# Attention in four-head units on a TensorE-bound decoder trunk: scores of even and odd heads in turn, and first loads in finer steps

## The chip, the cores and the metric

The kernel runs on one core of a Trainium2 chip. The metric is the device time of one execution in microseconds; the profile's span, from the first to the last instruction of the program, is a little shorter. TensorE does matmuls and transposes, VectorE (DVE) and ScalarE (ACT) do elementwise work, GpSimd (POOL) does a few powers and issues some DMAs, and SyncE (SP) issues nearly all loads.

## The reference

Two layers of a decoder trunk on 256 tokens of width 2048. Each layer normalises its input, projects it once, feeds the columns to a gated spatial unit (A) and to windowed attention (B), projects both back, and then runs a SwiGLU block:

```python
def swa_sink_attention(q, k, v, q_norm_g, k_norm_g, sinks, rel_bias):
    ...
    scores = jnp.einsum('bnqkgd,bnskd->bnkgqs', q, kb).astype(jnp.float32) * scale
    ...
    scores = jnp.where(valid[None, :, None, None], scores + bias, NEG_INF)
    sink = ...
    probs = jax.nn.softmax(jnp.concatenate([scores, sink], axis=-1), axis=-1)[..., :-1]
    out = jnp.einsum('bnkgqs,bnskd->bnqkgd', probs.astype(vb.dtype), vb)
...
for l in range(DEPTH):
    h = rms_norm(x, norm1_g[l])
    z = h @ w_in[l]
    z_sgu = jax.nn.gelu(z[..., :2 * SGU_WIDTH], approximate=False)
    out_a = chunked_sgu(z_sgu, sgu_norm_g[l], sgu_w[l], sgu_b[l])
    out_b = swa_sink_attention(...)
    mixed = jnp.concatenate([rms_norm(out_a, out_norm_a[l]),
                             rms_norm(out_b, out_norm_b[l])], axis=-1)
    x = x + mixed @ w_out[l]
    h2 = rms_norm(x, norm2_g[l])
    x = x + (jax.nn.silu(h2 @ w_gate[l]) * (h2 @ w_up[l])) @ w_down[l]
```

Attention has 16 query heads of width 64 in 4 key groups of 4 heads, and two query blocks of 128 tokens. The first block sees 128 keys, the second 256. Everything is float32.

## The kernel before

**The weight stream.** Every product takes its weights in tiles of 256 x 512 floats. SP loads a tile into `raw` (line 90), ScalarE casts it to a rounded high part `wh` (line 99), VectorE computes the rest `wl` (line 100), and TensorE makes three matmuls of 512 columns per part (`mm3`, lines 138 to 140). One such tile with its 12 matmuls is a *unit*, and a counter `clock[0]` advances by one tick per unit. All other work is put into the stream with `later(delay, fn)`, which runs `fn` once the counter has advanced far enough. So the order of the Python calls, refined by the scheduler that builds the program, sets the order on each engine.

**PSUM.** There are eight banks. `pa` has five, for the accumulators `acc` (each product uses two, one per token block). `pd` has two and `pm` one; small results (transposes, scores, probabilities) take a bank through `small_ps`, which goes round over `pm`, `pd`, `pd`.

**Attention.** In each layer the projection is done in blocks of 512 columns: keys and values first, then the first eight query heads (`in_block(4)`), then the others (`in_block(5)`), then the gate columns (`v_gate`, `u_gated`). From `in_block(5)` on, the stream carries attention between its units. There are 12 attention units per layer: for each key group one with the first query block and all four heads, one with the second block and the even heads (`par` = (0,)), and one with the second block and the odd heads. `attend` makes the scores (line 361), adds the bias into `s` (line 368), takes the maximum (373), the exponentials with their sums on ScalarE (381) and the reciprocal of the sum. Three ticks later `turn` transposes the probabilities into `pt` (lines 395 and 396), five ticks later `weigh` multiplies them with the values (line 402) into `ob` (line 412). `attend_end` transposes `ob` for the output projection. Even heads lie in partitions 0 to 63 and odd heads in partitions 64 to 127 of `qT` and `kT`, so a score matmul has 64 rows:

```python
nc.tensor.matmul(
    ps[:, i, :],
    qT[h // 8][HD * r : HD * r + HD, (h % 8) // 2, t * P : (t + 1) * P],
    kT[HD * r : HD * r + HD, g, :nk],
    start=True, stop=True,
)
```

**The spatial gate.** `v_gate` normalises v per head: squares and sums on VectorE, the power on POOL (`inv_rms`, line 186), and the products on VectorE again (lines 456 and 457), which wait for POOL.

**The start.** TensorE runs 12 matmuls on a constant tile (`heat`, line 169). SP first issues the constants `cst` (line 164), then two tiles of the transposed input (`first_pair`, line 241), then the first weights in halves.

Of the kernel before, what the change touches and what calls it, by code (L numbers as in the profile page):

```python
# [12 lines left out]
F32 = mybir.dt.float32  # L13
# [3 lines left out]
ALU = mybir.AluOpType  # L17
# [4 lines left out]
P = 128  # L22
# [4 lines left out]
HD = 64  # L27
NH = 16
NKV = 4
GRP = NH // NKV  # L30
# [6 lines left out]
KT = D // P  # L37
# [30 lines left out]
def trunk(ctx, tc, x, xt, w_in, w_out, w_gate, w_up, w_down, sgu_w, sgu_g, consts,  # L68
          rel_bias, onehot, radd, out):
    nc = tc.nc  # L70
# [4 lines left out]
    zp = ctx.enter_context(tc.tile_pool(name="zp", bufs=8))  # L75
    ap = ctx.enter_context(tc.tile_pool(name="ap", bufs=2))
    sp = ctx.enter_context(tc.tile_pool(name="sp", bufs=4))
    dp = ctx.enter_context(tc.tile_pool(name="dp", bufs=1, space=DRAM))
    pa = ctx.enter_context(tc.tile_pool(name="pa", bufs=5, space=PSUM))
    pd = ctx.enter_context(tc.tile_pool(name="pd", bufs=2, space=PSUM))  # L80
    pm = ctx.enter_context(tc.tile_pool(name="pm", bufs=1, space=PSUM))
# [36 lines left out]
    def later(delay, fn):  # L118
        pending.append((clock[0] + delay, next(serial), fn))
# [11 lines left out]
    turns = itertools.count()  # L131

    def small_ps(shape, name):
        pool, tag = ((pm, "sm"), (pd, "dacc"), (pd, "dacc"))[next(turns) % 3]
        return pool.tile(shape, F32, tag=tag, name=name)

    def mm3(acc, ah, al, wh, wl, first, last):
# [23 lines left out]
        return acc  # L161

    cst = cp.tile([P, L, C_L], F32, tag="cst", name="cst")
    nc.sync.dma_start(cst, consts)
    junk = zp.tile([P, NB], BF16, tag="z", name="junk")
    nc.vector.memset(junk, 1.0)
    heat = small_ps([P, NB], "heat")
# [6 lines left out]
    ident = cp.tile([P, P], F32, tag="ident", name="ident")  # L174
    make_identity(nc, ident)

    def small(shape, name):
        return sp.tile(shape, F32, tag=name, name=name)
# [15 lines left out]
    def split_gain(ps, lay, col, tag, spare=False):  # L194
        pair = pair_tile(tag, spare)
        for j in range(2):
            g = cst[:, lay, col + j : col + j + 1]
            nc.scalar.activation(pair[:, 0, j, :], ps[:, j, :], AF.Copy, scale=g)
            nc.vector.scalar_tensor_tensor(
                pair[:, 1, j, :], ps[:, j, :], g, f(pair[:, 0, j, :]), ALU.mult, ALU.subtract  # L200
            )
        return pair

    def transpose_pair(blocks, ps=None):
        ps = small_ps([P, 2, SEQ], "ps_t") if ps is None else ps
        for j in range(2):
            for t in range(NTOK):
                nc.tensor.transpose(
                    ps[:, j, t * P : (t + 1) * P], blocks[t][:, j * P : (j + 1) * P], ident
                )  # L210
        return ps

    def sum_sq(dst, src):
        void = zp.tile([P, NB], BF16, tag="z", name="void")
        nc.scalar.activation(void[:, : src.free_size()], src, AF.Square, accum_out=dst)
# [15 lines left out]
    def bc(a, n):  # L231
        return a.unsqueeze(2).to_broadcast([P, a.shape[1], n])
# [6 lines left out]
    def first_pair(p, pairs=pairs1):  # L239
        xr = zp.tile([P, 2, SEQ], F32, tag="z", name="xr")  # L240
        nc.sync.dma_start(xr, xt[:, 2 * p : 2 * p + 2, :])
        pairs.append(split_gain(xr, 0, C_G1 + 2 * p, "hT"))
# [22 lines left out]
        )  # L265
        nc.sync.dma_start(rdram, skew)

    for p in range(2):
        first_pair(p)
    for p in range(2, KT // 2):  # L270
        later(p - 1, lambda p=p: first_pair(p))
    for i in range(2 * NTOK):
        later(5 + 2 * i, lambda i=i: load_x(i // 2, i % 2))
    later(11, rel_table)
# [1 line left out]
    for lay in range(L):  # L276
        layer = {}

        def in_block(nb, lay=lay, pairs=pairs1):
            return product([w_in[lay, nb, c] for c in range(KT // 2)], pairs)  # L280
# [7 lines left out]
        zkv = []  # L288
        kT = ap.tile([P, NKV, SEQ], F32, tag="big", name="kT", bufs=8)

        def kv_norm(acc, lay=lay, layer=layer, zkv=zkv, kT=kT):
# [22 lines left out]
        qT = [  # L314
            ap.tile([P, 4, SEQ], F32, tag="big", name=f"qT{b}", bufs=8) for b in range(2)
        ]
# [22 lines left out]
        ob = {}  # L339
        bias = {}  # L340
        pairs_b = [None] * NKV

        def load_bias(g, bias=bias):
            bt = ap.tile([P, GRP, SEQ], F32, tag="big", name="bias", bufs=8)
            nc.gpsimd.dma_start(bt, rdram[g * GRP : (g + 1) * GRP].rearrange("h q k -> q h k"))
            bias[g] = bt

        def attend(g, t, par, zkv=zkv, kT=kT, qT=qT, ob=ob, bias=bias, layer=layer):
            nk = (t + 1) * P
            k0 = SEQ - nk  # L350
            nh = 2 * len(par)
            heads = [h for h in range(GRP) if h % 2 in par]
            step = heads[1] - heads[0]
            nkb = nk // P
            nsink = layer["nsink"]
            s = ap.tile([P, nh, nk], F32, tag="spt", name="s", bufs=4)
            for r in par:
                ps = small_ps([P, 2, nk], "ps_s")
                for i in range(2):
                    h = g * GRP + 2 * i + r  # L360
                    nc.tensor.matmul(  # L361
                        ps[:, i, :],
                        qT[h // 8][HD * r : HD * r + HD, (h % 8) // 2, t * P : (t + 1) * P],
                        kT[HD * r : HD * r + HD, g, :nk],
                        start=True,
                        stop=True,
                    )
                nc.vector.scalar_tensor_tensor(
                    s[:, par.index(r) :: len(par), :], ps, 1.0 / math.sqrt(HD),
                    bias[g][:, r::2, k0:], ALU.mult, ALU.add,  # L370
                )
            m = small([P, GRP], "m")[:, :nh]
            nc.vector.tensor_reduce(m, s, AX.X, ALU.max)
            hs = slice(g * GRP + heads[0], (g + 1) * GRP, step)
            nm = small([P, GRP], "nm")[:, :nh]
            nc.vector.scalar_tensor_tensor(nm, m, -1.0, nsink[:, hs], ALU.mult, ALU.min)
            es = small([P, GRP], "es")[:, :nh]
            nc.vector.tensor_tensor(es, nm, nsink[:, hs], ALU.subtract)
            den = small([P, GRP], "den")[:, :nh]
            for i in range(nh):  # L380
                nc.scalar.activation(
                    s[:, i, :], s[:, i, :], AF.Exp, bias=nm[:, i : i + 1],
                    accum_out=den[:, i : i + 1],
                )
            nc.scalar.activation(es, es, AF.Exp)
            rden = small([P, GRP], "rden")[:, :nh]
            nc.vector.tensor_tensor(rden, den, es, ALU.add)
            nc.vector.reciprocal(rden, rden)
            pt = ap.tile([P, nh * nkb, P], F32, tag="spt", name="pt", bufs=4)

            def turn():
                pst = small_ps([P, nh * nkb, P], "ps_p")
                s4 = s.rearrange("p h (b k) -> p (h b) k", k=P)
                for i in range(nh * nkb):
                    nc.tensor.transpose(pst[:, i, :], s4[:, i, :], ident)
                nc.vector.tensor_copy(pt, pst)

            def weigh():
                pv = small_ps([P, nh, HD], "ps_v")
                for i in range(nh):  # L400
                    for b in range(nkb):
                        nc.tensor.matmul(
                            pv[:, i, :],
                            pt[:, i * nkb + b, :],
                            zkv[b][:, (NKV + g) * HD : (NKV + g + 1) * HD],
                            start=b == 0,
                            stop=b == nkb - 1,
                        )
                if (g, t) not in ob:
                    ob[g, t] = zp.tile([P, GRP * HD], F32, tag="z", name="ob")  # L410
                o3 = ob[g, t].rearrange("p (h d) -> p h d", d=HD)
                nc.vector.tensor_tensor(o3[:, heads[0] :: step, :], pv, bc(rden, HD), ALU.mult)

            later(3, turn)
            later(5, weigh)

        def attend_end(g, lay=lay, ob=ob, ssb=ssb, pairs_b=pairs_b):
            for t in range(NTOK):
                sum_sq(ssb[t][:, g : g + 1], ob[g, t])
            ps = transpose_pair([ob[g, t] for t in range(NTOK)])  # L420
            pairs_b[g] = split_gain(ps, lay, C_GB + 2 * g, "aT", g >= 2)
# [106 lines left out]
        acc = in_block(4)  # L528
        load_bias(0)
        q_norm(0, acc)  # L530
        units = [(g, t, par) for g in range(NKV) for t, par in ((0, (0, 1)), (1, (0,)), (1, (1,)))]
        for i, (g, t, par) in enumerate(units):
            at = 6 + (9 * i) // 4
            later(at, lambda g=g, t=t, par=par: attend(g, t, par))
            if i % 3 == 2:
                if g + 1 < NKV:
                    later(at, lambda g=g: load_bias(g + 1))
                later(at + 7, lambda g=g: attend_end(g))
        layer["anchor"] = anchor[0]
        q_norm(1, in_block(5))  # L540
        for b in range(2):
# [276 lines left out]
```

## Time and profile before

| | |
|---|---|
| median of 3 runs | 1976.16 us (1975.98 to 1976.36) |
| the profiled execution | 1975.9 us |
| its span | 1974.1 us |
| TensorE busy | 1958.7 us |
| VectorE busy | 1664.9 us |
| ScalarE busy | 1137.7 us |
| GpSimd busy | 119.2 us |
| moved by DMA | 420.22 MB |

"Busy" is the union of the instructions of an engine; a matmul's end is modelled, and matmuls overlap in the pipeline, so the distance from one start to the next says what one costs, not the duration. A float32 matmul (scores, weighted sums) leaves two records.

### The profile page before, as it was taken

How to read it: one execution, taken by the hardware profiler on the slowest of the kernel's cores; microseconds unless marked ns; L12 is line 12 of the kernel's file. 1: busy time of each engine (PE TensorE's matmuls, PEld its weight loads, DVE VectorE, ACT ScalarE, POOL GpSimd, SP SyncE). 2: the span in 40 equal slices, each digit the busy share in tenths (PEclk: the TensorE clock that was granted, in tenths of full speed). 3: DMA queues.
4: the chain of work that ended last, by engine and by line, in shares of the span. 5: the costliest groups of instructions: out<-in, count | busy, mean ns of one | idle time of the engine just before them, and what ended most of it. 6: DMA issues, size and time to landing. Idle time of an engine off the chain costs nothing.

```text
span 1974.1 us, 24670 instructions
## 1 busy us (share of the span) xinstructions
PE 1958.7 (99%) x8942; PEld 1602.0 (81%) x8942; DVE 1664.9 (84%) x1931; ACT 1137.7 (58%) x1441; POOL 119.2 (6%) x129
## 2 busy tenths in 40 slices
PE   9999999999999999999999999999999999999999
PEld 6788888878878888888888788888888888888887
DVE  6777689989999898999667776899899898999984
ACT  6465566556656556656455655666556565565562
POOL 1211001000000000000002100000000000000000
PEclk9999999999999999999999999999999999999999
DMA  8753557776686776867655445586776867768773
GB/s 315 262 173 129 191 162 229 225 226 212 215 267 197 238 226 206 254 221 244 201 185 194 147 150 187 167 244 202 235 224 223 255 204 234 230 217 255 216 241 110
DMA packets 118554, 420.22 MB, mean 213 GB/s; under 512 B 13040, under 2 KB 15216, under 8 KB 118432
## 3 DMA queue, kind: packets, MB, share of 16 engines
q1 hardware_dynamic: 107072, 377.65, 55.4%
q0 software_dynamic: 11360, 41.00, 11.6%
q8 instruction: 70, 1.15, 0.2%
q14 instruction: 52, 0.43, 0.1%
HBM read 416.47 MB, written 4.23 MB: 213 GB/s over the span
## 4 chain that ended last, share of the span: by engine, by line
PE 87%; DVE 7%; DMA 3%; issue 2%; ACT 1%; POOL 0%; SPq 0%; ACTq 0%; POOLq 0%
PE dacc L138 10%; PE dacc L139 9%; PE dacc L140 9%; PE acc L138 9%; PE acc L140 9%; PE acc L139 9%; PE m L140 6%; PE m L139 6%; PE m L138 6%; DVE wl L100 3%; PE n L138 3%; PE n L140 3%; PE n L139 3%; DMA raw<-in_w_down_dram 1%; PE ps_s L361 1%
## 5 line engine op out<-in xcount | busy, mean ns | idle before, releaser
L99 ACT CAST wh<-raw 128x1024 fp32r<-128x1024 f32 (+1 forms) x770 | 793.8, 1049 | 652.6 <-PE acc L140 156.4
L100 DVE TENSOR_TENSOR wl<-raw,wh 128x1024 fp32r<-128x1024 f32 (+1 forms) x770 | 920.3, 1217 | 190.5 <-ACT wh L99 180.9
L138 PE MATMUL dacc<-wh,aT 128*128 128x512 f32 x576 | 225.1, 393 | 2.8 <-DVE xres L707 2.8
L139 PE MATMUL dacc<-wl,aT 128*128 128x512 f32 x576 | 225.0, 391 | 0.0
L140 PE MATMUL dacc<-wh,aT 128*128 128x512 f32 x576 | 224.8, 390 | 0.0
L139 PE MATMUL m<-wl,ext 128*128 128x512 f32 x512 | 200.6, 392 | 1.0 <-DVE wl L100 1.0
L138 PE MATMUL m<-wh,ext 128*128 128x512 f32 x512 | 200.1, 391 | 0.4 <-ACT wh L99 0.4
L140 PE MATMUL m<-wh,ext 128*128 128x512 f32 x512 | 199.4, 389 | 0.0
L138 PE MATMUL acc<-wh,hT 128*128 128x512 f32 x448 | 180.0, 404 | 1.0 <-ACT wh L99 1.0
L139 PE MATMUL acc<-wl,hT 128*128 128x512 f32 x448 | 175.4, 392 | 0.3 <-DVE wl L100 0.2
L140 PE MATMUL acc<-wh,hT 128*128 128x512 f32 x448 | 175.6, 392 | 0.0
L99 ACT CAST wh<-t 128x1024 fp32r<-128x1024 f32 x128 | 134.8, 1053 | 49.3 <-PE dacc L140 26.3
L100 DVE TENSOR_TENSOR wl<-t,wh 128x1024 fp32r<-128x1024 f32 x128 | 155.9, 1218 | 8.2 <-ACT wh L99 5.3
L138 PE MATMUL dacc<-wh,hT 128*128 128x512 f32 x384 | 151.2, 394 | 0.7 <-ACT sg L682 0.4
L138 PE MATMUL acc<-wh,aT 128*128 128x512 f32 x384 | 151.3, 394 | 0.0
L140 PE MATMUL acc<-wh,aT 128*128 128x512 f32 x384 | 149.9, 390 | 0.0
L140 PE MATMUL dacc<-wh,hT 128*128 128x512 f32 x384 | 149.7, 390 | 0.0
L139 PE MATMUL dacc<-wl,hT 128*128 128x512 f32 x384 | 149.7, 390 | 0.0
L139 PE MATMUL acc<-wl,aT 128*128 128x512 f32 x384 | 149.6, 390 | 0.0
L624 POOL DMA_DIRECT2D t<-in_w_gate_dram x64 | 54.6, 853 | 1335.7 <-DVE wl L100 767.3
L138 PEld LDWEIGHTS dacc<-wh,aT 128*128 128x128 f32 x576 | 107.7, 188 | 27.8 <-DVE xres L707 5.6
L139 PEld LDWEIGHTS dacc<-wl,aT 128*128 128x128 f32 x576 | 108.2, 188 | 22.9 <-DVE wl L100 0.8
(151 smaller groups left out, 3007.5 us busy)
## 6 DMA issues: line engine op xcount, KB each, us to landing
raw<-in_w_gate_dram SPq DMA_DIRECT2D x176, 512.0 KB, 5.5
raw<-in_w_up_dram SPq DMA_DIRECT2D x176, 512.0 KB, 4.5
raw<-in_w_down_dram SPq DMA_DIRECT2D x176, 512.0 KB, 4.6
raw<-in_w_in_dram SPq DMA_DIRECT2D x108, 512.0 KB, 4.5
raw<-in_w_out_dram SPq DMA_DIRECT2D x64, 512.0 KB, 3.3
t<-in_w_gate_dram POOLq DMA_DIRECT2D x64, 512.0 KB, 7.1
bias<-rdram POOLq DMA_DIRECT2D x8, 512.0 KB, 5.8
xr<-in_xt_dram SPq DMA_DIRECT2D x8, 256.0 KB, 5.6
```

The lines of the kernel that those rows point to most:

```text
L99: nc.scalar.copy(wh[:, j : j + step, :], src)
L100: nc.vector.tensor_tensor(wl[:, j : j + step, :], src, f(wh[:, j : j + step, :]), ALU.subtract)
L138: nc.tensor.matmul(acc, ah, wh, start=first, stop=False)
L139: nc.tensor.matmul(acc, ah, wl, start=False, stop=False)
L140: nc.tensor.matmul(acc, al, wh, start=False, stop=last)
L361: nc.tensor.matmul(ps[:, i, :], qT[h // 8][HD * r : HD * r + HD, (h % 8) // 2, t * P : (t + 1) * P], kT[HD * r : HD * r + HD, g, :nk], sta ...
L624: nc.gpsimd.dma_start(t2, w_gate[lay, b, i, 1], accum_op=ALU.add)
```

## The change

Four things change. `small_ps` goes round over four turns, the third of which takes one of the five accumulator banks. The constants are loaded from ScalarE's queue, and only the first input tile is issued ahead of the first weights; the others follow one per tick. Attention has 8 units per layer: a key group and a query block, always with all four heads; the score matmuls go through the heads in the order even, odd, even, odd, into a bank for each parity, and the bias is added after all four. The transposes of the second block are split into two steps one tick apart, and its weighted sum comes at 6 ticks. Times within the stream are set anew, and the bias of the next group is loaded two to three ticks sooner.

```diff
     def small_ps(shape, name):
-        pool, tag = ((pm, "sm"), (pd, "dacc"), (pd, "dacc"))[next(turns) % 3]
+        pool, tag = ((pm, "sm"), (pd, "dacc"), (pa, "acc"), (pd, "dacc"))[next(turns) % 4]
...
-    nc.sync.dma_start(cst, consts)
+    nc.scalar.dma_start(cst, consts)
...
-    for p in range(2):
-        first_pair(p)
-    for p in range(2, KT // 2):
-        later(p - 1, lambda p=p: first_pair(p))
+    first_pair(0)
+    for p in range(1, KT // 2):
+        later(p, lambda p=p: first_pair(p))
...
-        def attend(g, t, par, ...):
+        def attend(g, t, ...):
-            s = ap.tile([P, nh, nk], F32, tag="spt", name="s", bufs=4)
-            for r in par:
-                ps = small_ps([P, 2, nk], "ps_s")
-                for i in range(2):
+            s = ap.tile([P, GRP, nk], F32, tag="spt", name="s", bufs=4)
+            halves = [small_ps([P, 2, nk], "ps_s") for r in range(2)]
+            for i in range(2):
+                for r in range(2):
                     h = g * GRP + 2 * i + r
                     nc.tensor.matmul(
-                        ps[:, i, :],
+                        halves[r][:, i, :],
...
+            for r in range(2):
                 nc.vector.scalar_tensor_tensor(
-                    s[:, par.index(r) :: len(par), :], ps, 1.0 / math.sqrt(HD),
-                    bias[g][:, r::2, k0:], ALU.mult, ALU.add,
+                    s[:, r::2, :], halves[r], 1.0 / math.sqrt(HD), bias[g][:, r::2, k0:],
+                    ALU.mult, ALU.add,
                 )
...
-            def turn():
-                pst = small_ps([P, nh * nkb, P], "ps_p")
+            def turn(c):
+                pst = small_ps([P, GRP, P], "ps_p")
                 s4 = s.rearrange("p h (b k) -> p (h b) k", k=P)
-                for i in range(nh * nkb):
-                    nc.tensor.transpose(pst[:, i, :], s4[:, i, :], ident)
-                nc.vector.tensor_copy(pt, pst)
+                for i in range(GRP):
+                    nc.tensor.transpose(pst[:, i, :], s4[:, c * GRP + i, :], ident)
+                nc.vector.tensor_copy(pt[:, c * GRP : (c + 1) * GRP, :], pst)
...
-            later(3, turn)
-            later(5, weigh)
+            for c in range(nkb):
+                later(3 + c, lambda c=c: turn(c))
+            later(5 + t, weigh)
...
-        units = [(g, t, par) for g in range(NKV) for t, par in ((0, (0, 1)), (1, (0,)), (1, (1,)))]
-        for i, (g, t, par) in enumerate(units):
-            at = 6 + (9 * i) // 4
-            later(at, lambda g=g, t=t, par=par: attend(g, t, par))
-            if i % 3 == 2:
-                if g + 1 < NKV:
-                    later(at, lambda g=g: load_bias(g + 1))
-                later(at + 7, lambda g=g: attend_end(g))
+        for g in range(NKV):
+            at = 6 + (27 * g) // 4
+            later(at, lambda g=g: attend(g, 0))
+            at += 2
+            later(at, lambda g=g: attend(g, 1))
+            if g + 1 < NKV:
+                later(at, lambda g=g: load_bias(g + 1))
+            later(at + 8, lambda g=g: attend_end(g))
```

More of the change, by code (lines that the diff above doesn't have):

```diff
@@ L346, in load_bias, with attend @@
             bias[g] = bt
-        def attend(g, t, par, zkv=zkv, kT=kT, qT=qT, ob=ob, bias=bias, layer=layer):
-            nk = (t + 1) * P
+        def attend(g, t, zkv=zkv, kT=kT, qT=qT, ob=ob, bias=bias, layer=layer):
+            nkb = t + 1
+            nk = nkb * P
             k0 = SEQ - nk
[L351 to L354, printed above, removed]
             nsink = layer["nsink"]
-            s = ap.tile([P, nh, nk], F32, tag="spt", name="s", bufs=4)
-            for r in par:
-                ps = small_ps([P, 2, nk], "ps_s")
-                for i in range(2):
+            s = ap.tile([P, GRP, nk], F32, tag="spt", name="s", bufs=4)
+            halves = [small_ps([P, 2, nk], "ps_s") for r in range(2)]
+            for i in range(2):
+                for r in range(2):
                     h = g * GRP + 2 * i + r
                     nc.tensor.matmul(
-                        ps[:, i, :],
+                        halves[r][:, i, :],
                         qT[h // 8][HD * r : HD * r + HD, (h % 8) // 2, t * P : (t + 1) * P],
@@ L367, in attend @@
                     )
+            for r in range(2):
                 nc.vector.scalar_tensor_tensor(
-                    s[:, par.index(r) :: len(par), :], ps, 1.0 / math.sqrt(HD),
-                    bias[g][:, r::2, k0:], ALU.mult, ALU.add,
+                    s[:, r::2, :], halves[r], 1.0 / math.sqrt(HD), bias[g][:, r::2, k0:],
+                    ALU.mult, ALU.add,
                 )
-            m = small([P, GRP], "m")[:, :nh]
+            m = small([P, GRP], "m")
             nc.vector.tensor_reduce(m, s, AX.X, ALU.max)
-            hs = slice(g * GRP + heads[0], (g + 1) * GRP, step)
-            nm = small([P, GRP], "nm")[:, :nh]
+            hs = slice(g * GRP, (g + 1) * GRP)
+            nm = small([P, GRP], "nm")
             nc.vector.scalar_tensor_tensor(nm, m, -1.0, nsink[:, hs], ALU.mult, ALU.min)
-            es = small([P, GRP], "es")[:, :nh]
+            es = small([P, GRP], "es")
             nc.vector.tensor_tensor(es, nm, nsink[:, hs], ALU.subtract)
-            den = small([P, GRP], "den")[:, :nh]
-            for i in range(nh):
+            den = small([P, GRP], "den")
+            for i in range(GRP):
                 nc.scalar.activation(
@@ L385, in attend @@
             nc.scalar.activation(es, es, AF.Exp)
-            rden = small([P, GRP], "rden")[:, :nh]
+            rden = small([P, GRP], "rden")
             nc.vector.tensor_tensor(rden, den, es, ALU.add)
             nc.vector.reciprocal(rden, rden)
-            pt = ap.tile([P, nh * nkb, P], F32, tag="spt", name="pt", bufs=4)
-            def turn():
-                pst = small_ps([P, nh * nkb, P], "ps_p")
+            pt = ap.tile([P, GRP * nkb, P], F32, tag="spt", name="pt", bufs=4)
+            def turn(c):
+                pst = small_ps([P, GRP, P], "ps_p")
                 s4 = s.rearrange("p h (b k) -> p (h b) k", k=P)
-                for i in range(nh * nkb):
-                    nc.tensor.transpose(pst[:, i, :], s4[:, i, :], ident)
-                nc.vector.tensor_copy(pt, pst)
+                for i in range(GRP):
+                    nc.tensor.transpose(pst[:, i, :], s4[:, c * GRP + i, :], ident)
+                nc.vector.tensor_copy(pt[:, c * GRP : (c + 1) * GRP, :], pst)
             def weigh():
-                pv = small_ps([P, nh, HD], "ps_v")
-                for i in range(nh):
+                pv = small_ps([P, GRP, HD], "ps_v")
+                for i in range(GRP):
                     for b in range(nkb):
@@ L408, in weigh @@
                         )
-                if (g, t) not in ob:
-                    ob[g, t] = zp.tile([P, GRP * HD], F32, tag="z", name="ob")
+                ob[g, t] = zp.tile([P, GRP * HD], F32, tag="z", name="ob")
                 o3 = ob[g, t].rearrange("p (h d) -> p h d", d=HD)
-                nc.vector.tensor_tensor(o3[:, heads[0] :: step, :], pv, bc(rden, HD), ALU.mult)
-            later(3, turn)
-            later(5, weigh)
+                nc.vector.tensor_tensor(o3, pv, bc(rden, HD), ALU.mult)
+            for c in range(nkb):
+                later(3 + c, lambda c=c: turn(c))
+            later(5 + t, weigh)
         def attend_end(g, lay=lay, ob=ob, ssb=ssb, pairs_b=pairs_b):
```

## The prediction

> **What bounds the kernel now.** I read the page first (busy shares and the chain), then busy time by stage, TensorE's own waits, and last TensorE's timeline around single attention steps.
>
> ```profile
> span 1974.1 us, 24670 instructions
> PE 1958.7 (99%) x8942; PEld 1602.0 (81%) x8942; DVE 1664.9 (84%) x1931; ACT 1137.7 (58%) x1441; POOL 119.2 (6%) x129
> PE 87%; DVE 7%; DMA 3%; issue 2%; ACT 1%; POOL 0%; SPq 0%; ACTq 0%; POOLq 0%
> 58.00:200.00 142.00, 139.71 (x726) 112.64 (x725) 106.08 (x201) 79.60 (x163) 22.09 (x19) 1.00 0.54 185
> 1051.00:1200.00 149.00, 148.05 (x767) 120.44 (x766) 108.98 (x210) 85.98 (x174) 18.90 (x18) 1.00 0.51 164
> ```
>
> TensorE is the bound: 99% busy, and 87% of the chain that ended last. The last two rows are the stages of the two layers that hold attention (stretch, length, then busy PE, PEld, DVE, ACT, POOL). DVE has 106.1 us of work in 142 there and ACT 79.6, so both have room and TensorE has none: what it no longer spends in these stages should come off the end. Outside them and the first 20 us the instruction order of the two built programs is the same on every engine, so nothing else is priced.
>
> **1. The score matmuls.** Two score steps inside the stream of weight matmuls, first one with 256 keys (second query block), then one with 128 keys (first block):
>
> ```profile
> 1061.61 0.39 PE L139 MATMUL acc<-wl,hT 128*128 128x512 f32 x1
> 1061.84 0.39 PE L140 MATMUL acc<-wh,hT 128*128 128x512 f32 x1
> 1062.15 1.13 PE L361 MATMUL ps_s<-kT,qT 64*128 64x256 f32 x4
> 1063.21 0.50 PE L138 MATMUL acc<-wh,hT 128*128 128x512 f32 x1
> 1063.55 0.40 PE L139 MATMUL acc<-wl,hT 128*128 128x512 f32 x1
> ```
>
> ```profile
> 1077.10 0.39 PE L140 MATMUL acc<-wh,hT 128*128 128x512 f32 x1
> 1077.41 0.72 PE L361 MATMUL ps_s<-kT,qT 64*128 64x128 f32 x8
> 1078.07 0.50 PE L138 MATMUL acc<-wh,hT 128*128 128x512 f32 x1
> 1078.40 0.39 PE L139 MATMUL acc<-wl,hT 128*128 128x512 f32 x1
> ```
>
> ```profile
> L361 PE MATMUL ps_s<-kT,qT x128: 272/374/480, 64.0 to 1152.2; 64*128 64x128 f32 x64, 64*128 64x256 f32 x64
> ```
>
> Starts, not durations, are to be read: the stream runs at one start each 0.23 us (1061.61 to 1061.84). From the last weight matmul before the scores (1061.84) to the second one behind them (1063.55) pass 1.71 us, where two periods would be 0.46: this step costs the path 1.25 us. The step with 128 keys costs 1.30 - 0.46 = 0.84 us. Each score matmul leaves two records (128 records for 64 matmuls), so the first step is two matmuls of one parity of heads, the second is four of both parities.
>
> Between the first score start and the next weight matmul lie 1.06 us in the step of 4 x 256 columns and 0.66 us in the step of 8 x 128: 1024 columns each, yet the second is 0.40 us shorter. Even heads stand in partitions 0 to 63, odd heads in 64 to 127; I read the rows as two halves of the array that work side by side when a step holds both parities. Then the second step has only 512 columns one after the other, which gives a price of 0.40/512 = 0.78 ns a column and 0.26 us for entering and leaving.
>
> The change gives the second block all four heads in one step: 8 records of 256 columns, alternating in parity, in two banks. Side by side that is 4 x 256 columns, 1.06 us, the same 1.25 us as one of today's steps. Today there are 64/4 = 16 such steps; afterwards 8. Gain 8 x 1.25 = **10.0 us**, all of it on TensorE. The step with 128 keys keeps its count and, with both parities, its 0.84 us.
>
> The order within a step becomes even, odd, even, odd, where the row at 1077.41 is even, even, odd, odd. [...]
>
> **2. Waits for a bank.** Waits of TensorE (us in total, times, the longest):
>
> ```profile
> PE ps_p L395 <- DVE s L368: 1.1, 2, 0.6
> PE ps_s L361 <- DVE aT L199: 0.9, 1, 0.9
> PE ps_s L361 <- DVE qT L330: 0.6, 1, 0.6
> PE ps_p L395 <- DVE ob L412: 0.4, 1, 0.4
> ```
>
> Three of these four rows (1.1 + 0.9 + 0.4 = 2.4 us) wait for VectorE to empty a bank, not for data: the small tiles rotate over three banks. The change adds every fourth turn from the five accumulator banks, of which two products hold four at most. The bank then comes back a turn later. I take **2.0 us** gained (0 to 2.4). The wait on qT is for data and stays.
>
> **3. The start.**
>
> ```profile
> 1.52 5.21 PE L169 MATMUL heat<-junk 128*128 128x512 bf16 x12 [1.52 <-DVE mhalf L171]
> 5.48 1.71 ACT L198 ACTIVATE hT<-xr,cst 128x256 fp32r<-128x256 f32 x4 [3.18 <-DMA xr<-in_xt_dram]
> 7.09 0.60 ACT L99 CAST wh<-raw 128x512 fp32r<-128x512 f32 x1
> 7.75 0.73 PE L138 MATMUL acc<-wh,hT 128*128 128x512 f32 x2 [1.01 <-ACT wh L99]
> 0.81 0.38 SPq L164
> 1.72 4.30 DMA xr<-in_xt_dram
> 6.04 5.86 DMA raw<-in_w_in_dram
> ```
>
> The first weight matmul waits 1.01 us behind the warm-up (which ends at 6.73) for a cast that stood behind four activations. The last rows are the chain: DMA sets this stretch. The constants' DMA leaves SP's queue (0.38 us of issue) for ScalarE's, where it stands ahead of a table load while ScalarE idles 3.18 us before its first data: nothing. The second activation pair's 256 KB no longer stands ahead of the first weights. The bound is the warm-up, so at most 1.0 us; a slower arrival could leave 0.2. I take **0.8**, near the upper end, because 0.38 us of issue and one of the transfers are taken out of the chain that the rows show.
>
> **4. The rest of the unit.**
>
> ```profile
> L368 DVE SCALAR_TENSOR_TENSOR s<-ps_s,bias 128x512 f32<-128x512 f32 x16 | 10.9, 682 | 13.5 <-PE ps_s L361 13.5
> L373 DVE TENSOR_REDUCE m<-s 128x2 f32<-128x512 f32 x16 | 10.8, 676 | 0.0
> L381 ACT ACTIVATE s<-s,nm 128x256 f32<-128x256 f32 x32 | 16.0, 501 | 19.9 <-DVE nm L376 19.9
> L186 POOL TENSOR_TENSOR ir<-ms,mhalf 128x8 f32<-128x8 f32 x16 | 31.1, 1948 | 163.6 <-DVE ms L184 127.4 <-DVE rden L387 36.2
> ```
>
> Transposes (L395) and weighted sums (L402) keep their counts on TensorE: nothing. VectorE loses 48 small instructions (1933 against 1885 in the built programs). What gets longer is the chain from scores to probabilities: two bias steps (1.36), a reduce of twice the width (about 1.35, estimated as twice 0.68), then four exponentials instead of two (2.0): 4.7 us. The first transposes come 3 ticks of 12 matmuls later, 3 x 12 x 0.23 = 8.3 us. So it fits, if VectorE's queue is not held up by more than 3.6 us; nothing is charged. Bias loads move up by two to three ticks on POOL's queue; the built order puts one wm mask between two of the POOL powers (1.95 us each), with VectorE's normalisation of v waiting on them. The transposes behind that have two ticks of slack, so nothing is charged either, but this is where rival D would begin.
>
> **Sum.** 10.0 + 2.0 + 0.8 = 12.8 us. The profiled execution took 1975.9 us (1.8 us around its span); the median of the runs is 1976.16. Taken from the median: 1976.2 - 12.8 = **1963.4 us**. What a measurement of this kernel can tell from no change is about 0.2%, 4 us.
>
> **Rivals.** [...]
>
> *B, no overlap at 256 columns.* Then 8 x 256 columns take 0.26 + 2048 x 0.78 ns = 1.86 us, the step costs 2.05 instead of 2 x 1.25, and 8 x 0.45 = 3.6 us are gained: 12.8 - 6.4 = 6.4 in all, 1969.8. No row of today shows 256 columns of both parities, so it can't be excluded.
>
> *C, the change doesn't do what it says, as the second bank comes late.*
>
> ```profile
> 1105.91 1.05 PE L361 MATMUL ps_s<-kT,qT 64*128 64x128 f32 x8
> 1106.89 0.50 PE L138 MATMUL acc<-wh,hT 128*128 128x512 f32 x1
> ```
>
> Here the same step took 0.98 instead of 0.66 us: the odd half started when the even one was nearly done. At 256 columns that loses 0.64 us, in all eight 5.1: 1968.5. One of eight such steps shows it today, with three banks.
>
> *D, slower.* The longer chain falls behind VectorE's queue, where it waits twice for POOL's power around the v gate (2 x 1.95), and behind two casts' residuals: the slack of 3.6 us is used up, and TensorE stands at the transposes. To end 0.2% slower it must lose 12.8 + 4 = 16.8 us, 2.1 us in each of the eight longer units; at 2.5 us each it gives 1976.2 - 12.8 + 20 = 1983. For it: POOL's 1.95 us, and that VectorE is in order. Against it: no row of TensorE's waits names the exponentials today, and only two units in a layer meet the v gate.
>
> **How the numbers follow.** Forecast 0.75; A 0.07; B 0.06; C 0.05; D 0.05; the gain given back by a new wait elsewhere, within 0.2%: 0.02. Low end: all bounds at their best (10.0 + 2.4 + 1.0) plus the one late step of today (0.3) is 13.7, 1962.5; VectorE and ScalarE doing less could remove small waits not listed, so 1960.5. High end: A with nothing gained at the banks and 0.2 at the start is 8.6, 1967.6; C reaches 1968.5. Range 1960.5 to 1968.5. Faster by over 0.2%: forecast, A, B and C, less what B and C lose if further waits join them: 0.90. Same 0.05, slower 0.05.
>
> **What would show it.** Right: 8 score steps of 256 columns with x8 records and about 1.06 us from first start to the next weight matmul; TensorE's waits on s, aT and ob gone or below 0.5 us; the first weight matmul near 7.0; the two attention stages shorter by about 6 us each. [...]

## The result, and the profile after

The changed kernel takes 1963.75 us (median of 4, 1962.07 to 1964.13) where the kernel before took 1976.26 in the same comparison: ratio 0.9935, 95% interval 0.9918 to 0.9952. In two later comparisons, on chips 3 and 7, it took 1961.85 (ratio 0.9921, 0.9908 to 0.9935) and 1961.49 (0.993, 0.9917 to 0.9944). It is 12.5 to 15.5 us faster, and 1963.4 us was forecast.

The page of the changed kernel, then busy time in the stretches that hold the same weight matmuls as the two attention stretches shown before (start and end, length, busy PE, PEld, DVE, ACT, POOL with instruction counts, granted clock, DMA share, GB/s):

```profile
span 1962.1 us, 24613 instructions
PE 1947.1 (99%) x8942; PEld 1596.4 (81%) x8942; DVE 1660.7 (85%) x1883; ACT 1131.1 (58%) x1429; POOL 120.3 (6%) x129
PE 88%; DVE 7%; DMA 3%; issue 2%; ACT 1%; POOL 0%; SPq 0%; ACTq 0%; DVEq 0%
```

```profile
57.28:192.28 135.00, 134.15 (x726) 110.42 (x725) 104.66 (x177) 76.42 (x157) 21.90 (x19) 1.00 0.57 194
1044.23:1186.33 142.10, 142.10 (x766) 117.64 (x765) 106.68 (x186) 82.62 (x168) 20.05 (x18) 1.00 0.53 172
```

TensorE starts as many matmuls as before (8942) and is still the bound, with 11.6 us less busy time. The 726 matmuls of the first stretch took 142.00 us before and now 135.00; the second went from 149 to 142.10.

The score steps on TensorE's timeline (start, duration, engine, line, operation, tiles, count), one with 256 keys and one with 128 keys:

```profile
1054.64 0.39 PE L139 MATMUL acc<-wl,hT 128*128 128x512 f32 x1
1054.87 0.39 PE L140 MATMUL acc<-wh,hT 128*128 128x512 f32 x1
1055.19 1.13 PE L357 MATMUL ps_s<-kT,qT 64*128 64x256 f32 x8
1056.25 0.50 PE L138 MATMUL acc<-wh,hT 128*128 128x512 f32 x1
1056.59 0.40 PE L139 MATMUL acc<-wl,hT 128*128 128x512 f32 x1
...
1095.84 0.39 PE L140 MATMUL acc<-wh,hT 128*128 128x512 f32 x1
1096.16 0.71 PE L357 MATMUL ps_s<-kT,qT 64*128 64x128 f32 x8
1096.80 0.50 PE L138 MATMUL acc<-wh,hT 128*128 128x512 f32 x1
1097.14 0.39 PE L139 MATMUL acc<-wl,hT 128*128 128x512 f32 x1
```

Eight records of 256 columns now lie where four lay, in the same 1.06 us from the first score start to the next weight matmul (1055.19 to 1056.25). From 1054.87 to 1056.59 pass 1.72 us; less two periods of 0.23 the step costs 1.26. The 128-key step costs 1.30 - 0.46 = 0.84, as before.

TensorE's waits in the changed kernel (us in total, times, the longest):

```profile
PE dacc L138 <- DVE xres L704: 3.8, 4, 1.5
PE m L139 <- DVE wl L100: 1.1, 3, 0.6
PE dacc L138 <- ACT sg L679: 1.1, 1, 1.1
PE ps_s L357 <- DVE qT L329: 0.6, 1, 0.6
```

The three rows that waited for a bank (on `s`, `aT` and `ob`, 2.4 us) are gone. The wait for data, on `qT`, stands as it was. What remains belongs to the feed-forward stages and the output projection.

To see where the time came from, the start of the n-th weight matmul is read from both timelines: the kernel before's less the other's is the lead. What the lead gains (us) from one point to the next, in one trace of each kernel run (the last column is the difference of the spans):

| kernel | first weight matmul at | lead at matmul 96 | attention, layer 0 | up to attention of layer 1 | attention, layer 1 | rest | lead at the end |
|---|---|---|---|---|---|---|---|
| changed | 5.80 | 0.76 | 7.09 | -0.90 | 6.72 | -1.58 | 12.07 |
| changed, on chip 3 | 6.16 | 0.75 | 7.08 | 0.76 | 6.72 | 0.17 | 15.47 |
| changed, on chip 7 | 5.68 | 0.88 | 7.05 | -0.06 | 6.67 | -0.16 | 14.36 |
| scores a tick apart | 6.11 | 0.51 | 1.74 | 0.43 | 1.59 | -1.21 | 3.04 |
| order even, even, odd, odd | 6.27 | 0.89 | 6.23 | 1.27 | 5.55 | 0.03 | 13.96 |
| three turns | 5.95 | 0.93 | 5.09 | -0.23 | 3.10 | -1.00 | 7.87 |
| before, with the new start | 6.26 | 1.06 | -0.04 | 0.11 | 0.00 | -1.35 | -0.21 |
| before, with four turns | 7.59 | -1.35 | 1.91 | 0.01 | 0.68 | 0.30 | 1.54 |
| merged steps | 5.35 | 0.87 | 8.43 | 1.16 | 2.91 | -0.61 | 12.76 |
| merged, 7 ticks apart | 6.26 | 1.04 | 7.31 | 1.19 | 6.87 | -0.31 | 16.10 |

The kernel before has its first weight matmul at 7.75. It was traced once, so every row is a lead over that one trace. The attention columns hold 437 and 477 weight matmuls each.

### The profile page after: what moved, and what is told of

Its sections match the earlier page's. It is cut to its first block, busy times and chain, and to the rows that moved or that the text cites. A ratio compares the mean times of both kernels' runs of the same rounds, so it can differ in the third digit from the quotient of the medians.

```text
span 1962.1 us, 24613 instructions
## 1 busy us (share of the span) xinstructions
PE 1947.1 (99%) x8942; PEld 1596.4 (81%) x8942; DVE 1660.7 (85%) x1883; ACT 1131.1 (58%) x1429; POOL 120.3 (6%) x129
## 4 chain that ended last, share of the span: by engine, by line
PE 88%; DVE 7%; DMA 3%; issue 2%; ACT 1%; POOL 0%; SPq 0%; ACTq 0%; DVEq 0%
PE dacc L138 10%; PE dacc L139 10%; PE dacc L140 10%; PE acc L138 9%; PE acc L140 9%; PE acc L139 9%; PE m L140 6%; PE m L139 6%; PE m L138 6%; DVE wl L100 3%; PE n L140 3%; PE n L139 3%; PE n L138 3%; PE ps_v L399 1%; DMA raw<-in_w_in_dram 1%
```

## The experiments

**Is it the pairing of even and odd heads?** The changed kernel, with the odd heads' scores of the second block one tick behind the even ones. The softmax stays on four heads.

```diff
+            def scores(r):
+                half = small_ps([P, 2, nk], "ps_s")
+                ...                      # two matmuls of parity r, bias into s[:, r::2, :]
+            def rest():
+                scores(1)
+                ...                      # maximum, exponentials, turn, weigh as they were
+            scores(0)
+            if t == 0:
+                rest()
+            else:
+                later(1, rest)
```

> The changed kernel, but in the second query block the odd heads' scores come one tick after the even heads' scores, so that no step holds both halves of the array; softmax stays on four heads and runs one tick later. Theory (the gain is the pairing of the two halves): the 8 steps of 8 x 256 columns become 16 steps of 4 x 256 at 1.25 us each, 10.0 us more than the changed kernel's 1963.8: about 1973.8. Rival (the gain is fewer and wider softmax instructions on VectorE and ScalarE): within 2 us of 1963.8, since those instructions stay as they are in the changed kernel.

Measured: 1971.99 us (ratio to before 0.9976, 0.9967 to 0.9986). On TensorE's timeline:

```profile
79.23 0.39 PE L140 MATMUL acc<-wh,hT 128*128 128x512 f32 x1
79.54 1.13 PE L357 MATMUL ps_s<-kT,qT 64*128 64x256 f32 x4
80.60 0.50 PE L138 MATMUL acc<-wh,hT 128*128 128x512 f32 x1
80.94 0.40 PE L139 MATMUL acc<-wl,hT 128*128 128x512 f32 x1
```

Half as many records take the same 1.06 us, and there are 16 such steps again. The attention stages lose 5.35 and 5.13 us of their gain, 10.5 together, where 10.0 was expected. The pairing carries the change. Of the gain in these stages 3.3 us are left (1.74 + 1.59), little more than the 2.6 us of the fourth turn alone (below), so larger units without the pairing are worth little.

**Does the order in the step matter?** The changed kernel with its two loops exchanged.

```diff
-            for i in range(2):
-                for r in range(2):
+            for r in range(2):
+                for i in range(2):
```

> The changed kernel with the score matmuls in the order even, even, odd, odd instead of even, odd, even, odd, still one step for both. Theory (each half of the array works through its own matmuls, whatever the order): 1963.8 within 1 us, score steps with 256 keys at 1.26 us on the path. [...]

Measured: 1962.4 us (ratio 0.9933, 0.9921 to 0.9945). The step:

```profile
78.89 0.39 PE L140 MATMUL acc<-wh,hT 128*128 128x512 f32 x1
79.21 1.14 PE L357 MATMUL ps_s<-kT,qT 64*128 64x256 f32 x8
80.28 0.50 PE L138 MATMUL acc<-wh,hT 128*128 128x512 f32 x1
```

It is 1.07 us long (79.21 to 80.28). The alternation of the heads brings nothing that these steps show: what counts is that both parities stand in one step, each with a bank. The order does show where the odd half's bank comes late: with three turns (next experiment) the alternating order started two records and held back six, the second even head's among them. The attention gains are 0.9 and 1.2 us smaller than in the changed kernel, part of it from one 128-key step with a late odd half (1.40 us instead of 0.85) and two waits of the transposes that the trace puts down to a cast (1.0 us in all); the runs of the two kernels overlap in time.

**What is the fourth turn worth with the new units?** The changed kernel with the old rotation.

```diff
-        pool, tag = ((pm, "sm"), (pd, "dacc"), (pa, "acc"), (pd, "dacc"))[next(turns) % 4]
+        pool, tag = ((pm, "sm"), (pd, "dacc"), (pd, "dacc"))[next(turns) % 3]
```

> The changed kernel with small tiles going round over three banks as before. Theory of the prediction (the fourth turn saves waits for VectorE to empty a bank): between 2 and 3 us more than 1963.8, about 1966.3, with waits of TensorE on s, aT or ob back in its list. Rival (the units themselves removed those waits): within 0.7 us of 1963.8.

Measured: 1968.58 us (ratio 0.9963, 0.9951 to 0.9976). TensorE's waits, then its timeline:

```profile
PE ps_s L357 <- DVE pt L393: 2.8, 2, 1.4
PE ps_t L208 <- DVE s L365: 0.8, 1, 0.8
```

```profile
1098.74 0.39 PE L140 MATMUL acc<-wh,hT 128*128 128x512 f32 x1
1099.06 0.49 PE L357 MATMUL ps_s<-kT,qT 64*128 64x128 f32 x2
1100.95 0.71 PE L357 MATMUL ps_s<-kT,qT 64*128 64x128 f32 x6 [1.41 <-DVE pt L393]
1101.59 0.50 PE L138 MATMUL acc<-wh,hT 128*128 128x512 f32 x1
```

In the 128-key step the odd half has no bank until VectorE has copied `pt`: it starts 1.9 us behind the even half, in one step of each layer. The attention gains fall by 2.0 and 3.6 us, 5.6 together. That misses the 2 to 3 us that were expected, and the waits that came back are mostly on `pt`, not on `s`, `aT` or `ob`.

**The start alone, and the fourth turn alone,** each put into the kernel before:

```diff
-    nc.sync.dma_start(cst, consts)
+    nc.scalar.dma_start(cst, consts)
...
-    for p in range(2):
-        first_pair(p)
-    for p in range(2, KT // 2):
-        later(p - 1, lambda p=p: first_pair(p))
+    first_pair(0)
+    for p in range(1, KT // 2):
+        later(p, lambda p=p: first_pair(p))
```

> The kernel before with only the changed start: constants on ScalarE's queue, one input tile ahead of the first weights. Theory: 0.8 us less than 1976.3, as in the changed kernel, where 96 weight matmuls after the start the lead is 0.76 us; the first matmul starts near 5.8. Rival (the lead is given back to later waits in the two feed-forward stages): 1976.3, with the lead gone by the end.

Measured: 1975.26 us beside 1976.7 on that chip (ratio 0.9992, 0.9983 to 1.0001). Its time alone doesn't tell it from no change. Its trace has a lead of 1.06 us at matmul 96, which stays to the end of the second attention stage and is then used up by 1.35 us in the last stages, where TensorE's waits are 2.7 us in this trace and 1.4 in that of before.

```diff
-        pool, tag = ((pm, "sm"), (pd, "dacc"), (pd, "dacc"))[next(turns) % 3]
+        pool, tag = ((pm, "sm"), (pd, "dacc"), (pa, "acc"), (pd, "dacc"))[next(turns) % 4]
```

> The kernel before with only the fourth turn of small tiles through the accumulator banks. Theory of the prediction: TensorE's waits on s, aT and ob (2.4 us) go, and the one late step of 128 keys (0.3 us): 2.0 to 3.0 us less than the kernel before. Rival (the fourth turn pays only where a step needs two banks at once, as in the new units): within 1 us of the kernel before, with the waits still in TensorE's list.

Measured: 1973.76 us beside 1977.35 (ratio 0.9983, 0.9974 to 0.9991). Of TensorE's waits for a bank one is left, the first row (the second is the wait for data):

```profile
PE ps_s L361 <- DVE aT L199: 1.0, 1, 1.0
PE ps_s L361 <- DVE qT L330: 0.6, 1, 0.6
```

The attention stages gain 1.91 + 0.68 = 2.6 us, with the old units. That trace began 1.35 us behind the kernel before with the same start, so one trace can't settle a start of a microsecond.

**Could one step take both query blocks?** The changed kernel with the second block's scores in the same tick as the first block's, so that 128-key and 256-key matmuls follow each other.

```diff
             at = 6 + (27 * g) // 4
+            at += 1
             later(at, lambda g=g: attend(g, 0))
-            at += 2
             later(at, lambda g=g: attend(g, 1))
+            at += 1
```

> The changed kernel with the two query blocks of a key group in the same tick, so that their two score steps stand next to each other on TensorE. Theory (a step pays about 0.4 us for entering and leaving the use of half the rows, besides its columns): up to 8 x 0.4 = 3 us less than the changed kernel. Rival (four banks at once are too many): TensorE waits inside the step for VectorE to empty a bank, 1 us or more in each, and the time is 0 to 8 us more than the changed kernel.

Measured: 1963.19 us (ratio 0.993, 0.9917 to 0.9942), beside 1961.85 of the changed kernel on the same chip; the runs of the two overlap, and the up to 3 us that were expected did not come. Undisturbed merged steps cost 1.71 us where the two apart cost 0.84 + 1.26: some 0.4 less each. Layer 0 gains 8.43 us instead of 7.09, but layer 1 only 2.91. There, TensorE's waits show one row, its timeline what followed, and the stretches the granted clock (a mean over each stretch, the figure 0.62 and 0.50 behind POOL's):

```profile
PE ps_v L399 <- DVE s L365: 1.5, 1, 1.5
```

```profile
1068.17 0.39 PE L140 MATMUL acc<-wh,hT 128*128 128x512 f32 x1
1068.49 1.95 PE L357 MATMUL ps_s<-kT,qT 64*128 64x128 f32 x16
...
1075.96 0.63 PE L139 MATMUL acc<-wl,hT 128*128 128x512 f32 x1
1076.39 0.63 PE L140 MATMUL acc<-wh,hT 128*128 128x512 f32 x1
1076.82 0.63 PE L138 MATMUL acc<-wh,hT 128*128 128x512 f32 x1
```

```profile
1072.00:1075.00 3.00, 3.00 (x18) 3.00 (x19) 3.00 (x6) 0.38 (x2) 1.42 (x1) 0.62 1.02 412
1075.00:1079.00 4.00, 4.00 (x13) 3.23 (x12) 2.59 (x8) 2.17 (x13) 0.57 (x1) 0.50 1.03 388
```

The weighted sums of one group stood in the tick of the next group's scores and waited for a bank of these scores: VectorE had 2.35 us of residuals ahead of the bias step that empties it. After the wait TensorE ran at half the clock: weight matmuls started every 0.43 us instead of 0.23, up to 1079. Layer 1 gains 5.5 us less than layer 0. From the last weight matmul ahead of that step to the first behind it pass 7.2 us (1068.17 to 1075.39), 3.2 more than at the same place in layer 0, and some ten weight matmuls at 0.2 us more each add 2: this stretch holds nearly all of the difference.

**The changed kernel again, on chip 3:**

> The changed kernel once more, for its trace. Theory (what the trace loses in the feed-forward stages is chance from run to run): the attention stages gain 6.7 to 7.1 us each again, to 0.1 us, while the lead at the end of a feed-forward stage differs from that of the first trace by up to 1.5 us. Rival (VectorE and ScalarE take the lead back in these stages): the same 0.9 and 1.6 us lost in them again.

Measured: 1961.85 us. The attention gains repeat, 7.08 and 6.72, while the column up to the second attention stage reads 0.76 instead of -0.90 and the last one 0.17 instead of -1.58. The theory that VectorE or ScalarE always take part of the gain back in the feed-forward stages falls: those columns differ by up to 1.75 us between two executions of the same program, on two chips.

**Merged steps with the groups 7 ticks apart,** so that scores and weighted sums don't share a tick, and the changed kernel once more on the same chip:

```diff
-            at = 6 + (27 * g) // 4
-            at += 1
+            at = 7 + 7 * g
```

> The changed kernel, with both query blocks of a key group in the same tick (as in the merged experiment) and the groups 7 ticks apart instead of 6 to 7, so that no group's scores stand in the tick in which the group ahead of it is weighed. Theory: each of the eight merged steps saves 0.40 us, and the wait of 1.5 us at the weighted sums (with the slow matmuls behind it, some 4 us in all) goes: both attention stages 3 to 3.5 us shorter than in the changed kernel, that is a gain over the kernel before of 8 to 10.5 us in each; about 1960 us beside 1963.2 of the first merged kernel. Rival: the wait was not due to that collision, and one of over 1 us with slow matmuls behind it shows up again in one stage; then 1963 to 1964.

Measured: 1961.77 us (ratio 0.9925, 0.9913 to 0.9937). TensorE's waits and a merged step:

```profile
PE ps_v L399 <- DVE pt L393: 1.6, 2, 0.8
```

```profile
127.20 0.39 PE L140 MATMUL acc<-wh,hT 128*128 128x512 f32 x1
127.52 1.58 PE L357 MATMUL ps_s<-kT,qT 64*128 64x128 f32 x16
129.03 0.50 PE L138 MATMUL acc<-wh,hT 128*128 128x512 f32 x1
129.37 0.40 PE L139 MATMUL acc<-wl,hT 128*128 128x512 f32 x1
```

The long wait and the slow stretch are gone, but the weighted sums now wait 0.8 us in each layer for the copy of `pt`. The gains of 7.31 and 6.87 us miss the expected 8 to 10.5, and lie 0.2 to 0.3 above the changed kernel's in its trace on this chip. Four merged steps at 0.4 us less one wait of 0.8 would have given 0.8 a layer; where the other 0.6 went was not traced. In time the two can't be told apart.

> The changed kernel again, on the same chip as the one with merged steps 7 ticks apart. Theory: 1962 to 1964 us, attention stages shorter than before by 7.1 and 6.7 us as in its first two traces. Rival, that these stages vary as the feed-forward stages do: either of them off by more than 0.5 us.

Measured: 1961.49 us (1961.09 to 1964.28), attention gains 7.05 and 6.67: in three traces each agrees within 0.05 us.

## Why the prediction was right, step by step

**1. The score matmuls: right, mechanism and size.** 1.25 us were forecast for the new step, 1.26 measured; 16 such steps became 8, 10.0 us. Splitting the step again cost 10.5 us in the attention stages. Rival B falls with the row at 1055.19: it asked for 1.9 us from the first start to the next weight matmul, and it is 1.06. The chance of 0.07 for A and the high end of the range count on a longer step, with 1.6 us less gain in all (12.8 - 2.0 - 0.6 - 8.6). No run shows that term: the step took 1.06 us in the order even, odd, even, odd and 1.07 in the order even, even, odd, odd.

**2. The banks: right sign, too small, and one interaction missed.** The listed 2.4 us of waits went entirely, where 2.0 were taken. In starts of weight matmuls the four stalls behind these rows were some 3.0 us (0.94 + 0.76 + 0.60 + 0.72), more than the idle time that the rows list. The fourth turn alone was worth 2.6 us in the old units. In the new ones it is worth 5.6, because each unit asks for two banks at once: without it the odd half comes late as in rival C, though at 128-key steps, 1.9 us in each of two (3.8 of the 5.6). The step priced the turn by waits of the old schedule, and did not ask what the new one would wait for without it.

**3. The start: the amount came close, the bound was the wrong one.** 0.8 us was forecast, and the lead at matmul 96 is 0.75 to 0.88 in the changed kernel's three traces. But the first weight matmul came at 5.80, not near 7.0:

```profile
1.52 4.36 PE L169 MATMUL heat<-junk 128*128 128x512 bf16 x12 [1.52 <-DVE mhalf L171]
5.24 0.91 ACT L198 ACTIVATE hT<-xr,cst 128x256 fp32r<-128x256 f32 x2 [0.52 <-DMA xr<-in_xt_dram]
5.80 0.50 PE L138 MATMUL acc<-wh,hT 128*128 128x512 f32 x1
7.08 0.62 ACT L99 CAST wh<-raw 128x512 fp32r<-128x512 f32 x1 [0.93 <-DMA raw<-in_w_in_dram]
7.75 0.50 PE L138 MATMUL acc<-wh,hT 128*128 128x512 f32 x1 [0.24 <-ACT wh L99]
8.48 0.50 PE L139 MATMUL acc<-wl,hT 128*128 128x512 f32 x1 [0.22 <-DVE wl L100]
```

The step took the warm-up's end, 6.73 in the trace of before, as a fixed bound. Here the same 12 matmuls took 4.36 us instead of 5.21: they start 0.43 us apart at first, as all of them do in the trace of before, but from 4.85 on 0.22 apart. The lead of 1.95 at the first weight matmul (7.75 - 5.80) then shrank to 0.76, as the second half of the weights came late and the cast at 7.08 had waited for its DMA. What bounds this stretch is the arrival of data, as the chain in the prediction said. In the nine traces with the new start the first weight matmul lies anywhere from 5.35 to 6.27, and the lead at matmul 96 (0.51 to 1.06) does not follow it. How much the new start is worth stays open to about a microsecond: these are leads over one trace of the old start, and the other one, of the kernel with four turns, lay 1.35 us behind it.

**4. The rest of the unit: right.** Nothing was charged and no wait names the softmax. One unit of the second block, all engines' timeline:

```profile
1056.35 1.29 DVE L365 SCALAR_TENSOR_TENSOR s<-ps_s,bias 128x512 f32<-128x512 f32 x2 [0.32 <-PE ps_s L357]
1058.15 1.21 DVE L370 TENSOR_REDUCE m<-s 128x4 f32<-128x1024 f32 x1
1060.30 0.51 ACT L378 ACTIVATE s<-s,nm 128x256 f32<-128x256 f32 x1
1061.79 0.49 ACT L378 ACTIVATE s<-s,nm 128x256 f32<-128x256 f32 x1
1065.84 0.61 PE L392 MATMUL ps_p<-ident,s 128*128 128x128 f32 x4
```

From the bias step to the last exponential's end pass 5.9 us (1056.35 to 1062.28), not 4.7: the bias steps, the reduce and the exponentials took what was forecast or a little less, but VectorE's and ScalarE's queues put other work between. The transposes start 9.5 us behind the bias step, not 8.3, since TensorE's other work lies between the weight matmuls too. So the slack is 3.6 us, the figure of the prediction, by two differences that cancel. Rival D did not happen. The order on VectorE, which spoke for it, shows in the trace of before: the scores that started at 152.94 had made way for the weighted sums at 153.59, but their first bias step started at 157.53, behind a product for which VectorE stood idle 0.92 us until POOL's power was done.

```profile
152.94 0.72 PE L361 MATMUL ps_s<-kT,qT 64*128 64x128 f32 x8
153.59 1.10 PE L402 MATMUL ps_v<-zkv,pt 128*128 128x64 f32 x8
156.93 0.69 DVE L456 TENSOR_TENSOR v<-v,ir 128x512 f32<-128x512 f32 x1 [0.92 <-POOL ir L186]
157.53 0.42 DVE L368 SCALAR_TENSOR_TENSOR s<-ps_s,bias 128x256 f32<-128x256 f32 x1
```

**The sum.** 12.8 us were forecast. The attention stages gained 13.8 (7.09 + 6.72) and the start 0.8: 14.6, so the terms were 1.8 us short. Of these the banks account for 1.0 (3.0 - 2.0) and the late 128-key step quoted for rival C, which was not counted as a gain in the sum, for 0.3; some 0.5 is spread over small differences that were not traced. In the first trace the stages between and behind took 2.5 us away (0.90 + 1.58), which the other two traces of the same kernel do not repeat. So a forecast within 0.4 us of the first median was partly luck, two differences that cancelled; the comparisons on chips 3 and 7, at 15.5 and 14.4 us, stand nearer to the 14.6.

## What to carry to other kernels

Where a matmul uses half the rows of the array, look for one of the other half and put both in the same step, each with its own bank ready: here 8 records of both halves took the 1.06 us of 4 of one half, and 1.07 in the other order. When a step asks for more buffers at once, price the rotation by the new demand, not by the waits of the old schedule: the fourth turn was worth 2.6 us with the old units and 5.6 with the new ones. Split a gain by stage over the same instructions in two traces, and repeat the trace, before a loss elsewhere is explained.

## What the runs showed of the hardware

- The two halves of the array paired in either order within a step: 8 records of 256 columns took 1.06 us alternating and 1.07 us in blocks, where 4 records of one half took 1.06 too. A 128-key and a 256-key step cost 0.84 + 1.26 us apart and 1.71 merged: some 0.4 us saved, and what they go to was not shown.
- A stall of TensorE of 1.5 us, in the first trace of merged steps, was followed by half the granted clock: 0.62 as the mean of 1072 to 1075, 0.50 from 1075 to 1079, with weight matmuls 0.43 us apart. Two stalls of 1.4 us with three turns were not: the clock was 1.00 from 1098.70 to 1105.50, at and behind the second of them, and 1.0 as the mean of the whole execution. What decides between them stays open.
- The same 12 warm-up matmuls took 4.15 to 5.30 us over the eleven traces, as the change from starts 0.43 us apart to starts 0.22 apart came sooner or later: after seven starts in one trace, in four not within the twelve. A warm-up's end read from one trace of this kernel is uncertain by about a microsecond (5.30 - 4.15).
